# Two halves of 272 columns for the fourth query tile's selected and compressed keys

## The chip, the cores and the metric

The kernel runs on one core of one Trainium2 chip. The metric is the device time of one execution in microseconds (us); the time quoted for a kernel is the median of its runs. The profile comes from one further execution. Its engines are PE (matrix multiplication), PEld (loading of PE's stationary operand), DVE (vector engine), ACT (scalar engine), POOL (GpSimd) and SP (which issues most transfers).

## The reference

One decoder layer over 512 tokens of width 2048: a mixer with two head groups, cross attention over 256 memory tokens, and a SwiGLU. The change lies in the first head group, sparse attention with 8 query heads and 2 key/value heads. Each head attends to compressed blocks (31 of them), to selected blocks, and to a sliding window, with a distance penalty on each score. Cut to these three branches:

```python
s = jnp.einsum('bkgtd,bknd->bkgtn', qb, kc)                  # compressed
s = jnp.where(vis, s - sl5 * (t[:, None] - cmp_mid[None, :]), NEG)
p = jax.nn.softmax(s, axis=-1)
o_cmp = jnp.einsum('bkgtn,bknd->bkgtd', p, vc)
...
s = jnp.einsum('bkgtd,bktnsd->bkgtns', qb, ks_g)             # selected
s = jnp.where(ok, s - sl6 * (tt - pos), NEG)
o_slc = softmax over (n, s) of s, times vs_g
...
s = jnp.einsum('bkgtd,bksd->bkgts', qb, kw)                  # window
o_win = softmax of the masked s, times vw
return gb[..., 0:1] * o_cmp + gb[..., 1:2] * o_slc + gb[..., 2:3] * o_win
```

With 512 tokens, the 16 selected blocks of 64 are all 8 that exist and the window of 512 reaches every earlier token, so both branches are causal attention with different keys.

## The kernel before

**Number format.** Each fp32 operand is split into a high and a low part (`split`, line 158: ACT casts the high part, DVE subtracts it from the original to get the low one). A product is three matmuls: high x high, high x low, low x high (`mm3`).

**Query tiles.** The 512 tokens are four tiles of 128 (`i` from 0 to 3). Tile `i` sees `n = 128 * (i + 1)` keys of the selected branch (`b == 0`, in the tiles KS) and of the window branch (`b == 1`, in KV). The 32 columns ahead of the selected keys in KS hold the compressed keys. Tiles 0 to 2 get both from one product of 160, 288 and 416 columns. For tile 3 that would be 544 columns, and one PSUM bank holds 512; so its selected keys are one product of 512 columns, and its compressed keys a product of 32 that shares tile 0's bank.

**Behind each product.** ACT has written the scaled distances into the tile P beforehand (line 738). DVE adds them to the scores and takes the row minimum in one instruction (line 750, with a read of its accumulator), scales the minimum (751), and ACT takes the exponential with a row sum (752). For the compressed columns, DVE adds their distances and writes `pc` (`visible`, line 711). When all four tiles are through, `weigh_blocks` makes the compressed softmax (714 to 720), and `scale` multiplies P by the gate over the row sum (730). Later PE transposes P (775), ACT and DVE split it into PH and PL, and PE multiplies them with the values into the bank named o.

**Order.** PE runs what it is given in a fixed order, and two things make that order. In the program, work that has to wait runs as generators (`flows`): a generator says after how many ticks it goes on, and the projections of the dense stream tick, once per six matmuls of 512 columns. Head h is started by its projection (two projections of 8 ticks each pass per head: one of queries, one of gates), waits until head h - 1 is done scoring, and then yields two ticks per score tile (one in the last head), eight tiles in all. Its attention products wait for those of head h - 1. Behind the last two gate products (`w_r67`), `flows.drain()` lets what is still open run to its end; then comes the output projection, whose first two tiles (`begun`) are taken up to their fifteenth of sixteen products before the sixteenth, that of head 7. Then a scheduler places every instruction on its engine, by priority and by when it takes its inputs to be ready, so that the matmuls of the output projection stand between those of the drain.

**Banks.** PSUM's eight banks are three named mm, two s, two t and one o. Scores go to the two named s in turn.

**Transfers.** The sums of blocks of w_down are DMAs on POOL's queue (lines 143 and 145); each goes out at a fixed tick (`SUMS`). POOL also reloads head and gate tiles that were spilled (line 844, into KS buffers), and SP's queue loads the weights (188) and x (852).

Of the kernel before, what the change touches and what calls it, by code (L numbers as in the profile page):

```python
# [14 lines left out]
OP = mybir.AluOpType  # L15
AX = mybir.AxisListType

T = 512
# [41 lines left out]
def hybrid_block(ctx: ExitStack, tc: tile.TileContext, x_t, mem_t, sv, cmat, umask, w_a, w_r67, w_v, w_vg, w_v3,  # L60
                 w_vsw, w_gk2, w_c1, w_c2, w_out, w_cq, w_ck, w_cv, w_co, w_gu, w_down, y_t):
    nc = tc.nc
    V, S, G, PE = nc.vector, nc.scalar, nc.gpsimd, nc.tensor
# [11 lines left out]
    def sb(shape, tag, bufs, dt=F32):  # L75
        return (pool_b if tag in LATE else pool).tile(shape, dt, name=tag, tag=tag, bufs=bufs)

    def small(tag, bufs):
        return sb([128, 32], tag, bufs)

    def triple(tag):
        return small(tag, 2)[:, :3 * NT].rearrange("p (a i) -> p a i", i=NT)
# [4 lines left out]
    def bank(tag):  # L87
        return psp.tile([128, 512], F32, name=tag, tag=tag, bufs={"mm": 3, "s": 2, "t": 2, "o": 1}[tag])
# [3 lines left out]
    def row(tag, dt=F32):  # L92
        return sb([128, 512], tag, BUFS[tag], dt)
# [3 lines left out]
    def mm(*args, **kw):  # L97
        last_mm[0] = PE.matmul(*args, **kw)  # L98
# [56 lines left out]
    def split(hi, lo, src, gain=None):  # L155

        if gain is None:
            return S.copy(hi, src), V.tensor_sub(lo, src, hi)  # L158
        return (S.activation(hi, src, AF.Copy, scale=gain),
                V.scalar_tensor_tensor(lo, src, gain, hi, op0=OP.mult, op1=OP.subtract))  # L160
# [38 lines left out]
    def mm3(ps, lhs, rhs, start, stop, again=False):  # L199
        mm(ps, lhs[0], rhs[0], start=start, stop=False, skip_group_check=again)  # L200
        mm(ps, lhs[0], rhs[1], start=False, stop=False, skip_group_check=again)
        mm(ps, lhs[1], rhs[0], start=False, stop=stop, skip_group_check=again)

    def part(pair, a, n):
        return pair[0][:, a:a + n], pair[1][:, a:a + n]
# [25 lines left out]
    def inv_rms(dst, src, n, tmp):  # L231

        S.activation(dst, src, AF.Ln, bias=eps, scale=1.0 / n)
        S.activation(dst, dst, AF.Exp, scale=-0.5)
        S.activation(tmp, dst, AF.Square)
        V.scalar_tensor_tensor(tmp, src, n * EPS, tmp, op0=OP.add, op1=OP.mult)
        V.tensor_scalar(tmp, tmp, -0.5 / n, 1.5, op0=OP.mult, op1=OP.add)
        V.tensor_mul(dst, dst, tmp)
# [317 lines left out]
    for h in range(GH):  # L556
        qk = []
        flows.start(gla_head(h, qk))
        q, k = row("Q"), row("Q")
# [68 lines left out]
    keys = [[None, None], [None, None]]  # L628
# [49 lines left out]
    def nsa_head(h, ps):  # L678
        kv = h // 4
        slope = 2.0 ** -(h + 1)  # L680
        qn = row("Q", F32R), row("Q", F32R)
        split(*qn, ps, g_q)
        sq = row("n")
        S.activation(sq, ps, AF.Square)
        yield W_SUM
        pn = bank("s")
        for i in range(NT):
            mm(pn[:, i:i + 1], sq[:, 128 * i:128 * i + 128], one, start=True, stop=True)
        qs = triple("qs")
        sc, sl, neg = qs[:, 0], qs[:, 1], qs[:, 2]  # L690
        V.tensor_mul(neg, pn[:, :NT], rc2)
        inv_rms(sc, neg, 128, sl)
        V.tensor_mul(sc, sc, rc)
        V.reciprocal(sl, sc)
        V.tensor_scalar(sl, sl, slope, None, op0=OP.mult)
        V.tensor_scalar(neg, sc, -1.0, None, op0=OP.mult)
        yield W_NORM
        while not {"kc", ("k", 0, kv), ("k", 1, kv)} <= done or h and ("s", h - 1) not in done:
            yield 1
        sm = triple("sm")  # L700
        mn = triple("mn")
        cf = triple("cf")

        def coefficients(b):
            V.reciprocal(cf[:, b, :], sm[:, b, :])
            V.tensor_mul(cf[:, b, :], cf[:, b, :], gates[:, :, 3 * h + b])

        pc, pc3 = sb([128, NT, 32], "pc", 1), sb([128, NT, 3, 32], "pc3", 1)

        def visible(i, s):  # L710
            V.scalar_tensor_tensor(pc[:, i], cdist[:, 32 * i:32 * i + 32], sl[:, i:i + 1], s, op0=OP.mult, op1=OP.add)

        def weigh_blocks():
            V.tensor_reduce(mn[:, 0, :], pc, axis=AX.X, op=OP.min)
            V.tensor_sub(pc, mn[:, 0, :][:, :, None].to_broadcast([128, NT, 32]), pc)
            V.tensor_mul(pc, pc, sc[:, :, None].to_broadcast([128, NT, 32]))
            S.activation(pc, pc, AF.Exp)
            V.reduce_sum(sm[:, 0, :], pc, axis=AX.X)
            coefficients(0)
            V.tensor_mul(pc3, pc[:, :, None, :].to_broadcast([128, NT, 3, 32]),  # L720
                         cf[:, 0, :][:, :, None, None].to_broadcast([128, NT, 3, 32]))

        ps_ = []

        def scale(b):
            coefficients(1 + b)
            for i in range(NT):
                n = 128 * (i + 1)
                pi = ps_[b][:, POFF[i]:POFF[i] + n]
                V.tensor_scalar(pi, pi, cf[:, 1 + b, i:i + 1], None, op0=OP.mult)  # L730

        for b in range(2):
            p = sb([128, 1280], "P", 2)
            ps_.append(p)
            for i in range(NT):
                n = 128 * (i + 1)
                pi = p[:, POFF[i]:POFF[i] + n]
                S.activation(pi, dist[:, 512 - n:], AF.Copy, scale=sl[:, i:i + 1])
                s = bank("s")
                q = part(qn, 128 * i, 128)  # L740
                c = 32 if b == 0 and i < 3 else 0
                mm3(s[:, :c + n], q, part(keys[b][kv], 0 if b or c else 32, c + n), start=True, stop=True)
                if c and i == 0:
                    mm3(s[:, 160:192], part(qn, 384, 128), part(keys[0][kv], 0, 32), start=True, stop=True)
                    visible(3, s[:, 160:192])
                if c:
                    visible(i, s[:, :32])
                s = s[:, c:c + n]
                m = mn[:, 1 + b, i:i + 1]
                V.tensor_tensor_reduce(pi, s, pi, scale=1.0, scalar=3e38, op0=OP.add, op1=OP.min, accum_out=m)  # L750
                V.tensor_mul(m, m, sc[:, i:i + 1])
                S.activation(pi, pi, AF.Exp, bias=m, scale=neg[:, i:i + 1], accum_out=sm[:, 1 + b, i:i + 1])
                yield 2 if h < NH - 1 else 1
            if b == 0:
                weigh_blocks()
            scale(b)
        done.add(("s", h))

        while "vc" not in done or h and ("a", h - 1) not in done:
            yield 1  # L760
        pct = bank("t")
        for i in range(NT):
            PE.transpose(pct[:96, 128 * i:128 * i + 128], pc3[:, i].rearrange("p r n -> p (r n)"), ident)
        pcs = row("e", F32R)[:96]
        S.copy(pcs, pct[:96])
        V.tensor_sub(pcs[64:], pct[64:96], pcs[64:])
        o = None
        for b in range(2):
            pt = sb([128, 1280], "PH", PTB, F32R), sb([128, 1280], "PL", PTB, F32R)

            def turn(j):
                n = 128 * (NT - j)
                tp = bank("t")
                for i in range(j, NT):
                    PE.transpose(tp[:, 128 * (i - j):128 * (i - j) + 128],
                                 ps_[b][:, POFF[i] + 128 * j:POFF[i] + 128 * j + 128], ident)
                split(*part(pt, TOFF[j], n), tp[:, :n])

            def weigh(j):
                n = 128 * (NT - j)  # L780
                mm3(o[:, 128 * j:], part(vsw[j], 256 * b + 128 * kv, 128), part(pt, TOFF[j], n),
                    start=False, stop=b == 1 and j == NT - 1)

            turn(0)
            yield 2
            if b == 0:
                o = bank("o")
                mm(o, vc[:, 128 * kv:128 * kv + 128], pcs, start=True, stop=False)
            for j in range(1, NT):
                turn(j)  # L790
                weigh(j - 1)
                yield 2
            weigh(NT - 1)
        done.add(("a", h))
        t = row("st" if h < 4 else "M")
        S.copy(t, o)
        sq = row("on")
        S.activation(sq, t, AF.Square)
        pn = yield from column_sums(sq, T, "on", "t", W_SUM)
        r = row("on")  # L800
        inv_rms(r, pn, 128, row("on"))
        V.scalar_tensor_tensor(t, t, vec("g_nsa"), r, op0=OP.mult, op1=OP.mult)
        mix[h] = spill(t) if h < 4 else t
# [294 lines left out]
    for j in range(8):  # L1098
# [5 lines left out]
        for k, i in order if j < 7 else sorted(order, key=lambda o: o[1]):  # L1104
            kt = 2 * j + k
            mm3(acc_v[i], part(mem["v"][kt], 128 * i, 128), part(halves[j], 512 * k, 512),
                start=kt == 0, stop=kt == KT - 1)
# [568 lines left out]
```

## Time and profile before

| | |
|---|---|
| runs | 2321.61, 2326.07, 2322.61 us; median 2322.61 |
| profiled execution | 2317.59 us, its span 2315.8 |
| sparse-attention scores | 365.3 to 670.2 us of the span (line 750) |
| granted PE clock, mean | 0.999 |

A span is the time from the first to the last instruction. PE's matmuls overlap: an instruction's length holds its way through the array, so the distance from one start to the next is what a matmul costs. In the views below, L98 is the line at which every matmul is recorded; what it computes is told by the tile it writes (s: scores, o: attention output, t: transposes and sums, mm: projections).

### The profile page before, as it was taken

The page shows a single profiled execution, that of the slowest core. Times are in us where ns is not written, and L with a number is a line of the kernel's source. Part 1 is how long each engine was busy: PE and PEld are TensorE (multiplying, and loading weights), DVE is VectorE, ACT ScalarE, POOL GpSimd, SP SyncE. Part 2 cuts the span into 40 slices and gives each one's busy share as a digit, 9 for nine tenths or more (in the row PEclk, how much of TensorE's full clock was granted, in tenths as well). Part 3 has the DMA queues.
Part 4 walks back from the last instruction along what each step waited for, and adds up shares of the span by engine and source line. Part 5 has one row for each costly group of instructions (what it writes and reads, how often), then busy time and mean ns, then how long its engine had stood idle before and what let it go on. Part 6 is the DMA issues. An engine that isn't in the chain of part 4 may idle for free.

```text
span 2315.8 us, 29653 instructions
## 1 busy us (share of the span) xinstructions
PE 2291.5 (99%) x10868; PEld 1906.0 (82%) x10868; DVE 1676.3 (72%) x2556; ACT 1188.2 (51%) x1825; POOL 151.4 (7%) x224
## 2 busy tenths in 40 slices
PE   8999999999999999999999999999999999999999
PEld 7988888888888878778888888888888888888787
DVE  6477765677784436688888788878887876775685
ACT  6334444566673335575455445545554555444442
POOL 0011101011111100120000000000000000000000
PEclk9999999999999999999999999999999999999999
DMA  6576656466658754495455435544554497666674
GB/s 195 140 182 161 155 163 176 119 178 174 153 171 249 197 166 146 169 255 180 151 168 178 158 123 174 175 150 139 173 177 141 146 329 273 243 238 243 244 256 146
DMA packets 138018, 425.79 MB, mean 184 GB/s; under 512 B 14192, under 2 KB 34672, under 8 KB 134544
## 3 DMA queue, kind: packets, MB, share of 16 engines
q1 hardware_dynamic: 80752, 306.96, 39.1%
q0 software_dynamic: 31392, 88.36, 15.9%
q10 hardware_dynamic: 25728, 28.58, 3.5%
q8 instruction: 85, 1.39, 0.2%
q14 instruction: 61, 0.50, 0.1%
HBM read 382.42 MB, written 85.72 MB: 202 GB/s over the span
## 4 chain that ended last, share of the span: by engine, by line
PE 50%; DMA 2%; DVE 2%; issue 1%; ACT 0%; SPq 0%; DVEq 0%; POOLq 0%; ACTq 0%
PE mm L98 20%; PE t L98 13%; PE s L98 9%; PE o L98 7%; DMA raw<-w_down 1%; DVE ql L158 1%; PE s L1315 1%; DMA raw<-w_gu 1%; DMA raw<-td 0%; DMA PB<-h 0%; DVE raw L1453 0%; PE t L1484 0%; ACT qh L158 0%; DVE C L1494 0%; DVE C L1407 0%
## 5 line engine op out<-in xcount | busy, mean ns | idle before, releaser
L158 ACT CAST qh<-raw 128x1024 fp32r<-128x1024 f32 (+1 forms) x526 | 511.6, 981 | 542.5 <-PE o L98 165.1
L158 DVE TENSOR_TENSOR ql<-raw,qh 128x1024 fp32r<-128x1024 f32 (+1 forms) x526 | 591.7, 1133 | 142.4 <-PE mm L98 49.9
L98 PE MATMUL mm<-X,wh 128*128 128x512 f32 x1600 | 506.2, 396 | 0.0
L98 PEld LDWEIGHTS mm<-X,wh 128*128 128x128 f32 x1600 | 295.0, 189 | 56.7 <-issue 0.8
L98 PE MATMUL t<-qh,PB 128*128 128x512 f32 x968 | 335.8, 392 | 0.1
L98 PE MATMUL mm<-X,wl 128*128 128x512 f32 x800 | 314.4, 393 | 0.1
L98 PE MATMUL mm<-qh,PB 128*128 128x512 f32 x868 | 310.1, 390 | 0.2 <-DVE C L1494 0.2
L158 DVE TENSOR_TENSOR wl<-w,wh 128x1024 fp32r<-128x1024 f32 (+2 forms) x150 | 179.6, 1200 | 161.4 <-ACT wh L158 159.8
L158 ACT CAST wh<-w 128x1024 fp32r<-128x1024 f32 (+2 forms) x150 | 154.1, 1029 | 234.6 <-PE mm L98 168.3
L98 PE MATMUL s<-qh,PB 128*128 128x512 f32 x672 | 233.1, 391 | 1.0 <-DVE T L1494 0.9
L98 PE MATMUL mm<-qh,PA 128*128 128x512 f32 x640 | 221.8, 390 | 0.0
L98 PEld LDWEIGHTS t<-qh,PB 128*128 128x128 f32 x968 | 181.8, 188 | 37.7 <-DVE C L1409 0.8
L98 PEld LDWEIGHTS mm<-qh,PB 128*128 128x128 f32 x868 | 163.0, 188 | 34.4 <-DVE C L1494 0.6
L98 PE MATMUL t<-ql,PB 128*128 128x512 f32 x484 | 188.8, 390 | 1.1 <-DVE ql L158 1.1
L98 PE MATMUL o<-qh,PB 128*128 128x512 f32 x484 | 187.8, 390 | 0.0
L98 PEld LDWEIGHTS mm<-X,wl 128*128 128x128 f32 x800 | 150.8, 188 | 32.7 <-DVE wl L158 1.4
L98 PE MATMUL mm<-ql,PB 128*128 128x512 f32 x434 | 169.5, 391 | 3.7 <-DVE ql L158 3.7
L98 PEld LDWEIGHTS s<-qh,PB 128*128 128x128 f32 x672 | 126.1, 188 | 27.5 <-DVE T L1494 1.3
L98 PEld LDWEIGHTS mm<-qh,PA 128*128 128x128 f32 x640 | 120.2, 188 | 25.1
L98 PE MATMUL s<-ql,PB 128*128 128x512 f32 x336 | 131.4, 391 | 0.1
L98 PE MATMUL mm<-ql,PA 128*128 128x512 f32 x320 | 124.6, 389 | 0.0
L1230 DVE TENSOR_TENSOR raw<-raw 128x1024 f32<-128x1024 f32 x80 | 97.0, 1222 | 15.8 <-DMA raw<-w_gu 15.8
(488 smaller groups left out, 3462.0 us busy)
## 6 DMA issues: line engine op xcount, KB each, us to landing
raw<-w_gu SPq DMA_DIRECT2D x88, 768.0 KB, 4.2
raw<-w_gu SPq DMA_DIRECT2D x88, 512.0 KB, 3.4
raw<-w_down SPq DMA_DIRECT2D x88, 512.0 KB, 4.6
td<-w_down POOLq DMA_DIRECT2D x66, 512.0 KB, 6.6
w<-w_a SPq DMA_DIRECT2D x60, 512.0 KB, 4.2
raw<-td SPq DMA_DIRECT2D x22, 1024.0 KB, 4.8
PB<-h POOLq DMA_DIRECT2D x35, 512.0 KB, 4.6
h<-T ACTq DMA_DIRECT2D x66, 256.0 KB, 3.3
```

The source lines that it names most:

```text
L98: last_mm[0] = PE.matmul(*args, **kw)
L158: return S.copy(hi, src), V.tensor_sub(lo, src, hi)
L1230: V.tensor_sub(raw[:, 0:1024], raw[:, 0:1024], raw[:, 512:1536])
L1315: PE.transpose(ps[f][:, 128 * i:128 * i + 128], hs[i][:, c:c + 128], ident)
```

## The change

Tile 3 of the selected branch no longer has a product of its own for the compressed keys. Its 32 + 512 columns are cut into two products of 272 columns each, in two banks, with a yield of one tick between them. The first half holds the 32 compressed keys and the first 240 selected ones, the second half the other 272. DVE reduces each half by itself, the second into a new column `most`, and a minimum of the two follows. Tiles 0 to 2 and the window branch are computed as before.

```diff
@@ -700,6 +700,7 @@
         cf = triple("cf")
+        most = small("most", 1)
 
@@ -736,18 +737,25 @@
                 S.activation(pi, dist[:, 512 - n:], AF.Copy, scale=sl[:, i:i + 1])
-                s = bank("s")
                 q = part(qn, 128 * i, 128)
-                c = 32 if b == 0 and i < 3 else 0
-                mm3(s[:, :c + n], q, part(keys[b][kv], 0 if b or c else 32, c + n), start=True, stop=True)
-                if c and i == 0:
-                    mm3(s[:, 160:192], part(qn, 384, 128), part(keys[0][kv], 0, 32), start=True, stop=True)
-                    visible(3, s[:, 160:192])
-                if c:
-                    visible(i, s[:, :32])
-                s = s[:, c:c + n]
+                c = 0 if b else 32
                 m = mn[:, 1 + b, i:i + 1]
-                V.tensor_tensor_reduce(pi, s, pi, scale=1.0, scalar=3e38, op0=OP.add, op1=OP.min, accum_out=m)
+                cuts = (0, c + n) if c + n <= T else (0, 272, c + n)
+                for j, (x, y) in enumerate(zip(cuts, cuts[1:])):
+                    if j:
+                        yield 1
+                    s = bank("s")
+                    mm3(s[:, :y - x], q, part(keys[b][kv], x, y - x), start=True, stop=True)
+                    z = 0 if j else c
+                    if z:
+                        visible(i, s[:, :z])
+                    if j:
+                        least, m = m, most[:, :1]
+                    V.tensor_tensor_reduce(pi[:, x + z - c:y - c], s[:, z:y - x], pi[:, x + z - c:y - c],
+                                           scale=1.0, scalar=3e38, op0=OP.add, op1=OP.min, accum_out=m)
+                    if j:
+                        V.tensor_tensor(least, least, m, op=OP.min)
+                        m = least
                 V.tensor_mul(m, m, sc[:, i:i + 1])
                 S.activation(pi, pi, AF.Exp, bias=m, scale=neg[:, i:i + 1], accum_out=sm[:, 1 + b, i:i + 1])
                 yield 2 if h < NH - 1 else 1
```

The change adds 8 lines above what follows it, so line 750 of before is 754 after, 711 is 712, 751 is 759 and 818 is 826.

On PE, at the score tiles of head 0 (s: the score bank, KS: the keys, Q: the queries; rows with - stand in before only, with + in the changed kernel only), the first tile:

```order
 L98 MATMUL mm<-wh,X 128x512
 L98 MATMUL s<-KS,Q 128x160 x3
-L98 MATMUL s<-KS,Q 128x32 x3
 L98 MATMUL o<-wh,X 128x512
 L98 MATMUL o<-wl,X 128x512
```

The three small products of tile 3's compressed keys are gone from tile 0's bank. On PE, at the fourth tile of the same head:

```order
 L98 MATMUL mm<-wl,X 128x512
 L98 MATMUL mm<-wh,X 128x512
-L98 MATMUL s<-KS,Q 128x512 x3
+L98 MATMUL s<-KS,Q 128x272 x3
 L98 MATMUL o<-wh,X 128x512
 L98 MATMUL o<-wl,X 128x512
```

The first half stands where the product of 512 columns stood; the second half follows one tick later, behind six more matmuls of the dense stream, and everything behind it in the head moves by that tick.

On DVE, behind the last two gate products (q<-mm), in the drain, before the change (P: scores of the last head, mn: row minima, wl: low part of a weight tile, X: low part of a tile of the output projection's input):

```order
L818 TENSOR_TENSOR q_6276<-mm,rs 128x512
L818 TENSOR_TENSOR q_6286<-mm,rs 128x512
L158 TENSOR_TENSOR wl<-w,wh 128x1024
L750 ISA P,mn<-s,P 128x128
L750 ISA mn 128x1
L750 ISA P,mn<-s,P 128x256
L750 ISA mn 128x1
L751 TENSOR_TENSOR mn<-mn,qs 128x1
L158 TENSOR_TENSOR X<-KS,X 128x512
L751 TENSOR_TENSOR mn<-mn,qs 128x1
L750 ISA P,mn<-s,P 128x384
```

And at the same place in the changed kernel (pc: scores of the compressed keys):

```order
L826 TENSOR_TENSOR q_6250<-mm,rs 128x512
L158 TENSOR_TENSOR X<-M,X 128x512
L826 TENSOR_TENSOR q_6260<-mm,rs 128x512
L158 TENSOR_TENSOR wl<-w,wh 128x1024
L754 ISA P,mn<-s,P 128x128
L754 ISA mn 128x1
L754 ISA P,mn<-s,P 128x256
L754 ISA mn 128x1
L759 TENSOR_TENSOR mn<-mn,qs 128x1 x2
L712 SCALAR_TENSOR_TENSOR pc<-cm,qs,s 128x32
L754 ISA P,mn<-s,P 128x384
L754 ISA mn 128x1
```

The scores that stand behind the gate products were those of the last head's window branch; now they are those of its selected branch (the row that writes pc belongs to that one), and the window branch follows further down.

## The prediction

> **What bounds the kernel now.** I read the page first, for the busy shares and the chain of work that ended last.
>
> ```profile
> span 2315.8 us, 29653 instructions
> ...
> PE 2291.5 (99%) x10868; PEld 1906.0 (82%) x10868; DVE 1676.3 (72%) x2556; ACT 1188.2 (51%) x1825; POOL 151.4 (7%) x224
> ...
> PE 50%; DMA 2%; DVE 2%; issue 1%; ACT 0%; SPq 0%; DVEq 0%; POOLq 0%; ACTq 0%
> ```
>
> PE is the bound nearly everywhere, so an edit pays by the PE time that it takes out, and costs whatever PE then has to wait for. The average says nothing on the sparse-attention stage itself, so next I read the busy time of each engine in stretches of it.
>
> ```profile
> core 0: us, PE busy (x) PEld busy (x) DVE busy (x) ACT busy (x) POOL busy (x), PEclk, DMA share, GB/s
> 620.00:650.00 30.00, 30.00 (x162) 25.38 (x162) 22.91 (x72) 21.75 (x49) 3.94 (x6) 1.00 0.53 141
> 650.00:660.00 10.00, 9.90 (x53) 8.00 (x52) 8.38 (x29) 7.51 (x20) 1.07 (x2) 1.00 0.31 109
> 660.00:670.00 10.00, 10.00 (x50) 7.99 (x49) 9.69 (x25) 7.86 (x17) 2.68 (x5) 1.00 0.61 204
> 670.00:680.00 10.00, 10.00 (x53) 8.13 (x52) 9.45 (x23) 9.56 (x22) 1.08 (x2) 1.00 0.66 221
> 680.00:690.00 10.00, 10.00 (x57) 8.00 (x56) 7.71 (x16) 7.38 (x15) 0.00 (x0) 1.00 0.30 99
> ```
>
> PE has no gap (the columns are length, then busy time and count by engine), and its clock is granted in full. But while DVE has a quarter of its time free until 650, it is 94 to 97% busy from 660 to 680, and ACT nearly as much from 670. That is the drain: the projections that PE used as filler end at 665, and the last two heads finish beside the first output products. The stage has room for DVE work in its middle, and little at its end.
>
> **The change: PE.** Per head, three matmuls of 512 columns and three of 32 go; six of 272 come. PE's prices are distances between starts, since the matmuls overlap; so I read its timeline around two score blocks of one head (columns: start, length, engine, line, what, count).
>
> ```profile
> 640.93 0.60 PE L775 MATMUL t<-ident,P 128*128 128x128 f32 x4
> 641.29 0.82 PE L98 MATMUL s<-KS,Q 128*128 128x160 f32 x6
> 641.96 0.72 PE L98 MATMUL mm<-X,wh 128*128 128x512 f32 x2
> ...
> 642.75 0.62 PE L98 MATMUL mm<-X,wh 128*128 128x512 f32 x2
> 643.20 0.39 PE L98 MATMUL mm<-X,wl 128*128 128x512 f32 x1
> 643.42 0.56 PE L98 MATMUL s<-KS,Q 128*128 128x288 f32 x3
> 643.82 0.64 PE L98 MATMUL mm<-X,wh 128*128 128x512 f32 x2
> ...
> 656.20 0.45 PE L98 MATMUL s<-KV,Q 128*128 128x128 f32 x3
> 656.49 0.45 PE L98 MATMUL mm<-X,wl 128*128 128x512 f32 x1
> ```
>
> Three of 512 columns take 642.75 to 643.42, 0.225 us each; three of 288 take 0.40, 0.133 each; three of 128 take 0.29, 0.097 each. The row of six at 641.29 holds three of 160 columns and the three of 32, in 0.67. Between 128 and 288 columns 160 comes to 0.106, which leaves 0.117 for each of 32 columns: they cost as much as 128. 272 columns, by the slope between 288 and 512 (0.00041 a column), cost 0.126. A head so pays 3 x 0.225 + 3 x 0.117 = 1.03 us before and 6 x 0.126 = 0.76 after. The saving is 0.27 a head, **2.1 us** for eight; 1.7 if 32 columns cost only the 0.097 of 128.
>
> The Trainium skill, "TensorE: Matmul & The Clock Gate", section "Back-to-back issue gap", speaks against it: it gives columns / 2.4 GHz + 2.5 ns, with a floor of about 25 ns for small ones. By that rule the three small matmuls cost 0.075 us, a head saves under 0.03, and an estimate for the whole is 0.2 us. The six in 0.67 us disagree with it: by its own price of 69 ns for 160 columns, the three of 32 would still take 0.46.
>
> **The change: DVE.** One reduction of 512 columns becomes two, of 240 and 272, each with a read of its accumulator, and a minimum of two columns is added. The groups of DVE in the stage price it (count, then busy sum and mean ns).
>
> ```profile
> L750 DVE CUSTOM_DVE_ANT_0 P<-s,P 128x512 f32<-128x512 f32 x16 | 11.0, 686 | 0.8 <-ACT P L738 0.7
> L751 DVE TENSOR_TENSOR mn<-mn,qs 128x1 f32<-128x1 f32 x64 | 10.0, 157 | 1.3
> ...
> L750 DVE CUSTOM_DVE_ANT_0 P<-s,P 128x384 f32<-128x384 f32 x16 | 8.9, 554 | 2.2 <-PE s L98 2.1
> ...
> L711 DVE SCALAR_TENSOR_TENSOR pc<-cm,qs,s 128x32 f32<-128x32 f32 x32 | 7.4, 240 | 4.1 <-PE s L98 3.8
> ...
> L750 DVE CUSTOM_DVE_ANT_0 P<-s,P 128x256 f32<-128x256 f32 x16 | 6.7, 419 | 1.9 <-PE s L98 1.9
> ```
>
> From 256 to 512 columns a reduction grows by 267 ns, so it has 152 ns that don't depend on width. The split costs that once more, the minimum 157 and the read of the accumulator 84 (below): 0.39 us a head. For seven heads DVE's free quarter hides it; in the last it lies in the drain and is counted there. The four visibility rows (L711) stay four.
>
> The new wait: nine banks named s are taken where eight were, from two, and the second half's follows the first by one tick instead of two. PE's weight loads stand behind it. The view of line 750 says what that wait is worth.
>
> ```profile
> L750 DVE DVE_READ_ACCUMULATOR2_ANT mn<- x64: 76/84/91, 365.5 to 670.2; 128x1 f32 x64
> ...
>   PEld s L98: 2.9, 12
> ```
>
> 2.9 us in 12 waits over 64 banks. At the same 0.045 a bank eight more cost 0.4; nothing at best; at worst 0.24 a wait in each head, 1.9. I take **+0.4**, since the loads run ahead of PE.
>
> **The change: ticks.** The program counts filler in ticks, six matmuls of 512 columns each; a head yields two ticks per score tile. The added yield makes a head 17 ticks where two projections give 16, and head h+1 starts scoring when head h is done. Counting the yields, head 7 starts 6 ticks later (395, not 389), while the projections end at tick 400 either way; the drain has 30 ticks, not 24. So 36 matmuls, 8.1 us, no longer lie beside the last head. In the drain the order of DVE above shows it: behind the last gate product only head 7's window scores were left; now most of its selected scores stand there too. The trace of before prices the drain from that product (L818) to the last of head 7's transposed low parts (PL at 689.24).
>
> ```profile
> 665.00 1.29 DVE L818 TENSOR_TENSOR q<-mm,rs 128x512 f32<-128x512 f32 x2
> 666.19 1.22 DVE L158 TENSOR_TENSOR wl<-w,wh 128x1024 fp32r<-128x1024 f32 x1
> 667.33 0.29 DVE L750 CUSTOM_DVE_ANT_0 P<-s,P 128x128 f32<-128x128 f32 x1
> ...
> 672.61 1.27 DVE L730 TENSOR_SCALAR P<-P,cf 128x128 f32<-128x128 f32 x4
> 673.80 1.21 DVE L158 TENSOR_TENSOR wl<-w,wh 128x1024 fp32r<-128x1024 f32 x1
> ...
> 689.24 0.28 DVE L158 TENSOR_TENSOR PL<-t,PH 128x128 fp32r<-128x128 f32 x1
> ```
>
> ```profile
> 665.00:689.50 24.50, 24.50 (x130) 19.86 (x128) 21.35 (x50) 21.55 (x45) 2.59 (x5) 1.00 0.54 182
> ```
>
> The order of after has 38 DVE rows more between these two: five reductions with their reads and column products 2.3 us (starts lie 0.08 closer than lengths), four scalings 1.2 (672.61 to 673.80), four splits of 512 columns 2.4 (0.60 each, as at 665.00), one weight split 1.1, three low parts 1.3, and the compressed branch's softmax and coefficients about 2.0, an estimate from L711 and columns. That is 10.3 us. PE has 11 filler matmuls more (2.5), fifteen score matmuls (2.0), nine of attention (1.3, at the score prices) and eight transposes (0.7, at the 0.09 of 640.93): 6.5 us. So PE needs 24.5 + 6.5 = 31.0, and DVE 21.35 + 10.3 = 31.65. DVE becomes the bound of the drain. If none of its 3.15 idle us stay, PE waits 0.65; if all do, 3.8. I take **+3.0**: DVE and ACT hand each block back and forth, both are over 87% busy, so the idle time between hand-overs is more likely to stay.
>
> Behind the drain comes head 7's norm, which ends in the split that the sixteenth product of two output tiles reads.
>
> ```profile
> 691.98 1.23 DVE L158 TENSOR_TENSOR wl<-w,wh 128x1024 fp32r<-128x1024 f32 x1 [1.26 <-PE mm L98]
> 693.13 0.68 DVE L158 TENSOR_TENSOR on<-on 128x512 fp32r<-128x512 f32 x1
> ```
>
> PE has 38 matmuls of cover there, 8.6 us, where it had 43. The chain loses as much: the weight split that held DVE until 693.13 has moved ahead of it. Zero, up to 1.1 if the split is late again.
>
> **The change: transfers.** The sums of w_down on POOL's queue go out at fixed ticks, so behind the drain each goes out 6 ticks earlier against the work. One now stands ahead of the last two reloads of spilled tiles (KS). By the prices above, DVE uses these some 8 us after their buffers come free, and they land in 2.9.
>
> ```profile
> td<-w_down POOLq DMA_DIRECT2D x5, 512.0 KB, 5.6
> td<-td POOLq DMA_DIRECT2D x4, 512.0 KB, 8.2
> KS<-spill POOLq DMA_DIRECT2D x6, 256.0 KB, 2.9
> ```
>
> Even queued behind a whole copy of 5.6 they are just in time: zero, at most 0.5. On SP's queue a load of x moves ahead of two of w_out that aren't read before the drain's end: zero. The memory-key stage, where PE does wait, meets copies and sums in another phase.
>
> ```profile
> 800.00:820.00 20.00, 17.88 (x77) 14.20 (x76) 7.11 (x7) 6.29 (x6) 2.23 (x3) 1.00 0.76 211
> 820.00:840.00 20.00, 17.24 (x73) 13.71 (x72) 8.72 (x15) 9.20 (x26) 1.68 (x2) 0.91 0.60 178
> ```
>
> PE is idle 2.1 + 2.8 = 4.9 us there. As many transfers fall into it as before; I take zero, between -4.9 (it vanishes) and +2.6 (one sum of 8.2 in place of a copy of 5.6).
>
> **The sum.** -2.1 + 0.4 + 3.0 = **+1.3 us**. The profiled execution took 2317.59, so 2318.9 for its like; the median of the runs is 2322.61, so I predict **2323.9**. The measurement can tell 0.2%, 4.6 us, from no change: below 2318.0 is faster, above 2327.3 slower.
>
> **Rivals.**
> - The saving stands alone: DVE works without gaps in the drain and no bank is waited for: -2.1 + 0.65 = -1.5, 2321.2. For it: 75% load ahead of the drain, so DVE arrives with nothing owed. Against it: ACT's 21.55 of 24.50.
> - The cover that is lost is lost in full: the order on PE is fixed, and in it head 7's first transposes and products now follow each other with no filler between, so all 36 matmuls of cover come back as waits: -2.1 + 0.4 + 8.1 = +6.4, 2329.0, **slower**. It decides once the drain's wait passes 6.3 us. For it: DVE at 97% from 660; against it: DVE's own sum asks for 3.8 at most.
> - The change doesn't do what it says: 272 columns don't hide the weight load, and each matmul costs the 0.188 of a load's mean, which the page has.
>
> ```profile
> L98 PEld LDWEIGHTS s<-qh,PB 128*128 128x128 f32 x672 | 126.1, 188 | 27.5 <-DVE T L1494 1.3
> ```
>
>   Then a head pays 1.13, not 0.76: +0.8 in place of -2.1, +4.2 in all, 2326.8. Against it: 0.133 for 288 columns in the same place.
> - The shifted sums clear the memory-key stage and the drain holds: -1.5 - 4.9 = -6.4, 2316.2, faster. Against it: the transfers there are as many.
>
> **How the numbers follow.** The forecast has 0.47, the saving alone 0.22, the unhidden loads 0.06; all three lie within 0.2%: same 0.75. Lost cover 0.16 is slower, the cleared stage 0.09 faster. The range runs from 2319.5 (the saving alone, less 1.7, half of what the highest of the runs, 2326.07, lies above their median) to 2329.0, the price of lost cover; it leaves out the cleared stage and the part of lost cover beyond its price.
>
> **What would show it.** Score rows of 272 columns about 0.126 us apart, with none of 32. DVE over 95% busy in the 30 us behind the last gate product, and PE idle for 1 to 4 us there, before DVE's low parts or ACT's casts. If PE is idle for over 6, the lost cover is right; if for none, the saving alone. The memory-key stage should still be idle for about 5; if it isn't, the prediction falls by a cause beside the drain.

## The result, and the profile after

The changed kernel takes 2339.77 us (median of five runs, 2338.16 to 2344.15) against 2322.61: 1.008 times the time of the kernel before, interval 1.0068 to 1.0091. It is slower by some 17 us; 2323.9 was predicted, and 2329.0 was the end of the range. Its profiled execution has this page (span, then busy time by engine):

```profile
span 2337.5 us, 29690 instructions
...
PE 2306.4 (99%) x10868; PEld 1909.3 (82%) x10868; DVE 1675.8 (72%) x2580; ACT 1189.6 (51%) x1825; POOL 151.7 (6%) x224
```

The span is 21.7 us longer, and PE, with as many matmuls, is busy for 14.9 of them. So most of the loss is not idle time: the matmuls themselves are longer, or stand further apart. The steps that were predicted come first.

**The scores.** The timeline of PE at the two halves of head 0's fourth tile:

```profile
376.85 0.53 PE L98 MATMUL s<-KS,Q 128*128 128x272 f32 x3
377.22 0.40 PE L98 MATMUL o<-wh,X 128*128 128x512 f32 x1
...
378.61 0.54 PE L98 MATMUL s<-KS,Q 128*128 128x272 f32 x3
378.99 0.39 PE L98 MATMUL mm<-wh,X 128*128 128x512 f32 x1
```

Three matmuls of 272 columns take 0.37 and 0.38 us, that is about 0.125 each, where 0.126 was predicted. The 272-column step is right.

**The drain.** Busy time in its stretches (columns as before: length, then each engine, granted clock, transfers):

```profile
660.00:670.00 10.00, 10.00 (x53) 8.38 (x53) 8.02 (x15) 5.84 (x11) 0.00 (x0) 1.00 0.16 53
670.00:680.00 10.00, 8.79 (x45) 6.70 (x43) 8.97 (x37) 8.64 (x21) 1.91 (x4) 1.00 0.41 133
680.00:690.00 10.00, 7.85 (x43) 6.45 (x44) 8.47 (x27) 8.97 (x22) 1.84 (x4) 0.98 0.60 183
690.00:700.00 10.00, 10.00 (x44) 8.14 (x44) 6.98 (x12) 6.30 (x12) 1.08 (x2) 0.84 0.44 132
```

PE is idle for 1.21 + 2.15 = 3.36 us from 670 to 690, where it was busy throughout before. The waits of PE from 640 to 700 name them (total, times, longest); the same view of the kernel before has no row at all:

```profile
PE o L98 <- ACT X L158: 2.1, 1, 2.1
PE o L98 <- DVE PL L158: 1.4, 2, 1.2
```

The second row is a low part of P for which PE waits, as foreseen. The first row's releaser has to be checked, since a wait for several things is put down to the last. The timeline at its end (last column: idle time before the instruction, and who ended it):

```profile
687.04 1.27 DVE L731 TENSOR_SCALAR P<-P,cf 128x128 f32<-128x128 f32 x4
...
688.35 0.69 DVE L774 TENSOR_TENSOR e<-t,e 32x512 fp32r<-32x512 f32 x1
688.45 0.61 ACT L158 CAST X<-KS 128x512 fp32r<-128x512 f32 x1
...
689.18 0.47 PE L98 MATMUL o<-e,vc 96*128 96x512 f32 x1 [2.10 <-ACT X L158]
```

The matmul reads e. Its low part ends on DVE at 689.04, and ACT's cast of X happens to end at 689.06. So the wait is DVE's: the compressed branch's e stands in DVE's queue behind the four scalings of the window branch. And then something that no term of the sum had. The windows of 1 us around this wait (the clock granted to PE is the last number but two):

```profile
687.00:688.00 1.00, 0.08 (x1) 0.00 (x0) 0.96 (x5) 1.00 (x4) 0.29 (x1) 1.00 0.51 182
688.00:689.00 1.00, 0.00 (x0) 0.00 (x0) 0.97 (x2) 1.00 (x4) 0.00 (x0) 1.00 0.99 201
689.00:690.00 1.00, 0.82 (x5) 0.78 (x6) 0.97 (x3) 1.00 (x3) 0.00 (x0) 0.85 0.78 311
690.00:691.00 1.00, 1.00 (x4) 0.81 (x4) 1.00 (x3) 0.59 (x2) 0.35 (x1) 0.50 0.01 4
691.00:692.00 1.00, 1.00 (x3) 0.77 (x3) 1.00 (x2) 0.00 (x0) 0.19 (x1) 0.50 0.24 37
692.00:693.00 1.00, 1.00 (x4) 0.85 (x3) 0.02 (x1) 0.00 (x0) 0.45 (x1) 0.50 0.69 217
693.00:694.00 1.00, 1.00 (x8) 0.86 (x7) 0.00 (x0) 0.96 (x2) 0.08 (x1) 0.94 0.22 29
```

Behind 2.1 idle us the clock stands at 0.50 for 3.4 us, and PE does 3 or 4 matmuls per us in place of the 5 to 9 it did from 680 to 687. Added up, (1 - 0.85) + 3 x 0.50 + (1 - 0.94) = 1.7 us of clock are lost: the wait costs nearly twice its length.

**The memory-key stage.** Its windows, of the kernel before and then of the changed one:

```profile
800.00:960.00 160.00, 153.95 (x727) 127.23 (x726) 87.33 (x157) 78.46 (x151) 9.91 (x15) 0.99 0.47 148
```

```profile
800.00:960.00 160.00, 154.34 (x711) 126.67 (x710) 81.58 (x141) 72.53 (x137) 9.68 (x14) 0.99 0.49 150
```

PE is idle for 6.05 us before and 5.66 after. It is not the place.

**Where the time goes.** The start of the n-th matmul record can be compared between the profiles, since both have 10868 of them. How far the changed kernel lies behind, in us:

```
matmul        400   1600   3200   3600   4800   last
lag           1.7    3.3    8.3   13.8   17.6   21.7
before, at   79.6  291.6  606.5  683.9  950.2  2311.2
```

(The profiled execution of before lies 5.0 us under its median, so the last number is larger than the 17 of the medians. Behind matmul 4800, 3.1 of the 4.1 us come near 1045 us, where the clock of the changed kernel falls to one half for 3.41 us once more; the profile of before has no such spell there, but three kernels below that are as fast as before have one (256 idle bytes, both idle tiles, ticks shared out), so the change need not be its cause.) Three things are in this row. From 3200 to 3600, the drain, the lag grows by 5.5. But it has grown to 3.3 before the first score is multiplied (365 us), where the order of the instructions is the same, and it goes on growing behind the drain. So I looked at the distance of matmuls where both kernels do the same, near 20 us. Of the kernel before, the start of a product o<-wh,X and that of the one 12 matmuls later:

```profile
20.20 0.39 PE L98 MATMUL o<-wh,X 128*128 128x512 f32 x1
...
22.92 0.39 PE L98 MATMUL o<-wh,X 128*128 128x512 f32 x1
```

And of the changed kernel:

```profile
20.77 0.40 PE L98 MATMUL o<-wh,X 128*128 128x512 f32 x1
...
23.55 0.40 PE L98 MATMUL o<-wh,X 128*128 128x512 f32 x1
```

12 matmuls take 2.72 us before and 2.78 after, 0.227 and 0.232 each, at a clock of 1.00 in both. That holds for the matmuls of 512 columns that read X and the weight tiles wh and wl, the last of which starts at 904 us before and at 922 after; those behind, which read other tiles, are 227 ns apart in both kernels. The trace has 2784 of them. What can touch them all is where the tiles lie. The added tile `most` takes 128 bytes per partition in the pool that wh and wl come from; it moved wh from address 134016 to 133888, that is from 128 bytes past a multiple of 256 to a multiple of 256, and wl likewise. X, in another pool, stayed at 128 bytes past one.

### The profile page after: what moved, and what is told of

The parts are those of the page before. It is cut to its first block, busy times and chain, and to the rows that moved or that the text cites. A ratio compares the mean times of both kernels' runs of the same rounds, so it can differ in the third digit from the quotient of the medians.

```text
span 2337.5 us, 29690 instructions
## 1 busy us (share of the span) xinstructions
PE 2306.4 (99%) x10868; PEld 1909.3 (82%) x10868; DVE 1675.8 (72%) x2580; ACT 1189.6 (51%) x1825; POOL 151.7 (6%) x224
## 4 chain that ended last, share of the span: by engine, by line
PE 91%; DVE 3%; DMA 2%; ACT 2%; issue 2%; ACTq 0%; SPq 0%; POOL 0%; DVEq 0%; POOLq 0%
PE mm L98 50%; PE t L98 15%; PE s L98 14%; PE o L98 9%; PE s L1323 1%; DMA w<-w_out 1%; PE t L783 1%; DVE ql L158 1%; ACT wh L158 1%; DVE wl L158 1%; DMA w<-w_ck 0%; DMA raw<-w_gu 0%; DMA w<-w_c 0%; ACT P L760 0%; DMA PB<-h 0%
## 5 line engine op out<-in xcount | busy, mean ns | idle before, releaser
L98 PE MATMUL mm<-X,wh 128*128 128x512 f32 x1600 | 511.8, 400 | 0.0
```

## The experiments

Two theories were to be told apart, and what each is worth: **the address** (the tile `most`, through the place of wh and wl) and **the order** (the split, and the tick between its halves). Ratios are to the kernel before, run on the same chip; its medians there were 2320.7 to 2321.6.

**Order without address.** The changed kernel, with `most` taken from an unused column of mn, so that no tile moves:

```diff
-        mn = triple("mn")
+        mn = small("mn", 2)
+        most = mn[:, 12:13]
+        mn = mn[:, :12].rearrange("p (a i) -> p a i", i=NT)
         cf = triple("cf")
-        most = small("most", 1)
...
-                        least, m = m, most[:, :1]
+                        least, m = m, most
```

> The changed kernel with its column for the second minimum taken from the unused end of the tile mn, so that no tile is added and every other tile stands at the address it had before the change; the order on each engine is that of the changed kernel. Address theory (the added tile moves one pool by 128 bytes, and matmuls that read it step at 232 ns instead of 227): about 14 us come back, 2324 to 2327 us, matmuls of 512 columns 227 ns apart in the first 950 us, and what is left, 1 to 5 us over before, is the drain. Order theory (all of the loss is the new order: drain, banks, transfers): 2338 to 2341 us, 232 ns apart as in the changed kernel.

Measured: 2330.32 us, ratio 1.0039 (1.0025 to 1.0053); 512-column matmuls 227 ns apart again. About half of the loss is gone with the address, and the order costs about 9 us; the time lies between the two theories, so both things cost.

**Address without order.** The kernel before with the idle tile, and then with one of twice its size:

```diff
+        small("most", 1)
```

> The kernel before with a tile of 128 bytes per partition added in the same pool and read by nothing; no instruction differs. Address theory: 2335 to 2338 us (2,600 matmuls of 512 columns that read the weight tiles wh and wl, 5 ns each, is 13 to 14 us), 232 ns apart. Order theory: 2322 to 2323 us, 227 ns.

```diff
+        sb([128, 64], "most", 1)
```

> As the run before, but the idle tile has 256 bytes. If the place within 256 bytes is what counts, wh and wl are back at 128 beyond a multiple of 256, and the time is that of before, 2321 to 2325 us, at 227 ns. If a longer stretch counts (512 bytes or more), or any shift at all, it is slow: 2334 us or more, at 230 ns or more.

Measured: 2329.01, ratio 1.0033 (1.0021 to 1.0046), for 128 bytes; 2322.59, 1.0007 (0.9996 to 1.0019), for 256. A tile that nobody reads costs 7.4 us, if it moves the others by 128 bytes, and nothing if by 256. That is half of the 13 to 14 us that were expected. In the profiles the distances behind the 2784 matmuls that read X against wh or wl come to 661.4 us, against 654.6 with 256 bytes: 6.8 us more, near the 7.4. Their median grows by 5 ns, but their mean only by 2.5: with 256 bytes a third of them stood 228 ns apart or more already. The two ratios, 1.0039 and 1.0033, come to 1.0072, at the lower end of the interval of the whole change.

**Whose address.** The kernel before with an idle tile ahead of X in its pool; then with both idle tiles:

```diff
+    pool_b.tile([128, 32], F32, name="lead")
```

> The kernel before with an idle tile of 128 bytes at the head of the other pool, so that X (the other operand of most of these matmuls) moves to a multiple of 256 and wh and wl stay 128 beyond one. Theory 'the weights' own place counts': 2321 to 2325 us, 227 ns. Theory 'the two operands must lie alike within 256 bytes': slow, 2334 to 2338 us, 232 ns. Theory 'no operand may start at a multiple of 256': slow as well.

```diff
+    pool_b.tile([128, 32], F32, name="lead")
...
+        small("most", 1)
```

> The kernel before with both idle tiles, one of 128 bytes at the head of X's pool and one of 128 bytes in the pool of wh and wl; no instruction differs. X, wh and wl then all stand at multiples of 256 bytes (in the kernel before, X and the weight tiles alternate: X 128 beyond, wh at 128, wl at 128). Theory A, that the operands of a matmul must stand alike within 256 bytes: the 512-column matmuls step at 227 ns as in the kernel before, time 2321 to 2325. Theory B, that no operand may stand at a multiple of 256 bytes: they step at 232 or more, time 2329 to 2337. If each operand costs by itself, the pitch is above 232, about 237, and the time 2335 to 2340.

Measured: 2330.11, 1.0038 (1.0024 to 1.0052), with X moved alone (the 2334 and more that were expected rest on the same 13 to 14 us); 2320.93, 1.0001 (0.9991 to 1.0011), with X and the weights moved. The median distances, worked out from the traces, with the tiles' places within 256 bytes:

```
                         X    wh,wl  qh,ql   mm<-X,wh   mm<-X,qh
before                 128      128    128     227 ns     227 ns
changed                128        0    128     232        227
before + 128           128        0    128     232        227
before + 256           128      128    128     227        227
before, X moved          0      128    128     232        231
before, both moved       0        0    128     227        231
```

The last row settles it within one kernel: X at 0 is fast with weights at 0, and slow with qh at 128. Neither place is bad by itself; the two operands have to lie alike. The kernel before has a few that bear it out: M stands at 0, and the 24 matmuls of 512 columns that read it against wh or wl, at 128, have medians of 232.5 and 230.5 ns. For matmuls that read KV or KS no such difference stands out of their scatter, and shifts other than 128 were not tried.

**The tick, and the halves.** What the order costs can come from the tick, which makes a head 17 ticks long, or from the halves. The tick alone in the kernel before; the changed kernel (without the tile) with no tick between its halves; and with tile 3's two ticks shared out, so that a head has 16 again:

```diff
+                if b == 0 and i == 3:
+                    yield 1
                 s = bank("s")
```

> The kernel before with one yield of one tick ahead of tile 3's scores in the first branch, and nothing else: 512 and 32 columns as before, no added tile. Theory A (the tick): 2330 to 2334, that is the +8.7 of the run without the tile, and 1.6 us more because the saving on the columns isn't there. Theory B (the halves): 2321 to 2325, as the kernel before.

```diff
-                    if j:
-                        yield 1
```

> The changed kernel without the added tile (most lies in an unused column of mn) and without the added yield between the halves: tile 3's second half stands directly behind its first, and the flows get as many ticks as in the kernel before. Theory A, that the +8.7 us left over in the run without the tile come from the added tick (work of the last head pushed behind the last gate product): 2319 to 2323, the PE saving of 1.6 us remains, less a wait for the second bank. Theory B, that they come from the halves themselves (more DVE and PE rows per head, more rounds of the score banks): still 2328 to 2332.

```diff
-                yield 2 if h < NH - 1 else 1
+                yield 2 if h < NH - 1 and len(cuts) == 2 else 1
```

> The changed kernel without the added tile and with tile 3's two ticks shared out, one between the halves and one behind them, so that a head takes as many ticks as before, but for the last one, which takes one more. Theory A (the ticks of all heads together push work behind the last gate product): most of the 8.7 us go, about 2321 to 2325; what the last head's one further tick costs remains, at most 2 us. Theory B (the halves themselves): still 2328 to 2332.

> The same kernel as the run with tile 3's ticks shared out (no added tile, one tick between the halves and one behind), in more rounds: it should lie at 2319 to 2322, and the interval tells whether the 1.6 us of PE's saving are there (ratio 0.9993) or not (1.000 or more).

Measured: the tick alone 2329.82, 1.0046 (1.0031 to 1.0061); no tick 2325.57, 1.0020 (1.0009 to 1.0031); ticks shared out 2319.05, 1.0003 (0.9992 to 1.0013), and in the second measurement 2320.40, 0.9998 (0.9989 to 1.0006). The tick alone costs what the whole order costs; the halves with 16 ticks cost nothing that can be told from noise. The kernel with no tick lies between its two theories. The waits of PE with the tick alone, from 640 to 700, and two windows:

```profile
PE o L98 <- DVE PL L158: 2.0, 2, 1.8
PE mm L98 <- ACT X L158: 0.7, 1, 0.7
PE s L98 <- DVE mn L752: 0.2, 1, 0.2
```

```profile
670.00:675.00 5.00, 2.58 (x15) 1.69 (x13) 5.00 (x14) 2.97 (x7) 1.07 (x2) 1.00 0.18 52
675.00:680.00 5.00, 5.00 (x19) 3.99 (x18) 3.45 (x6) 2.34 (x5) 2.15 (x4) 0.66 0.74 234
```

The drain of the changed kernel again, without its halves: PE waits while DVE is busy for 5.00 of 5.00, and then has 0.66 of its clock for 5 us (1.7 us lost). With the ticks shared out the same stretch has no gap:

```profile
670.00:675.00 5.00, 5.00 (x24) 4.04 (x23) 4.36 (x13) 5.00 (x12) 0.54 (x1) 1.00 0.68 231
675.00:680.00 5.00, 5.00 (x31) 4.07 (x31) 4.86 (x10) 4.62 (x10) 0.54 (x1) 1.00 0.65 217
```

The last head has one tick more than before in that kernel too, and it costs nothing; so it is the ticks that add up over the heads. Halves directly behind each other cost 4.9 us by the medians: there PE waits for a score bank that DVE hasn't read yet, five times between 370 and 700, and once for a weight tile, 2.8 us together:

```profile
PE s L98 <- DVE mn L753: 1.5, 5, 0.3
PE mm L98 <- ACT wh L158: 1.3, 1, 1.3
...
```

The other 2 us were not located.

**A tick less.** If a tick costs time, one less might bring some. The kernel before with one tick fewer per head, and the changed kernel (without the tile) with the tick between the halves and none behind:

```diff
-                yield 2 if h < NH - 1 else 1
+                yield 2 if h < NH - 1 and (b or i < 3) else 1
```

> The kernel before with one tick after tile 3's scores in the first branch where it has two: 15 ticks per head, nothing else. Theory A (a tick per head more costs because the last head's work then ends behind the last gate product, where nothing covers it): a tick less can give back only what the kernel before itself loses there, 0 to 1 us by its profile (PE busy 419.44 of 420 us from 300 to 720), and takes cover from each head's own norms: 2320 to 2324. Theory B (each tick costs by itself, about 9 us a tick per head): 2312 to 2316.

```diff
-                yield 2 if h < NH - 1 else 1
+                if len(cuts) == 2:
+                    yield 2 if h < NH - 1 else 1
```

> The changed kernel without the added tile, with one tick between tile 3's halves and none behind them: 15 ticks per head. Theory A: as the run with the ticks shared out, 2319 to 2323, or some us more if tile 3's reductions then lie too near the block weights that wait for them. Theory B (each tick costs by itself): 2310 to 2314.

Measured: 2329.05, 1.0036 (1.0022 to 1.0050), and 2332.89, 1.0053 (1.0039 to 1.0067). Both theories fall here: with 15 ticks the kernel is 8.1 and 11.9 us slower; with 17 it was 9.1 and 8.7. The waits of the first, from 370 to 700, lie elsewhere, before score banks and weight parts:

```profile
PE s L98 <- DVE mn L750: 1.1, 3, 0.6
PE mm L98 <- DVE wl L158: 1.1, 2, 0.8
PE o L98 <- DVE PL L158: 0.5, 2, 0.2
PE o L98 <- DVE e L766: 0.2, 1, 0.2
```

So it isn't that later is worse. Two projections give a head 16 ticks; a head of 15 or 17 moves by one tick against the projections with each head, and each would come to its own collisions. That 16 is the good count was measured; that the step of the projections is why, is argued. The waits listed add up to some 3 us of 8; the rest is spread over distances that the view of waits doesn't count, and was not located.

## Why the prediction was wrong

**The step that failed** is "The change: DVE": it priced "a minimum of two columns is added" as 157 ns, and the column `most` that it needs at nothing; that it moves wh and wl by 128 bytes, and that this lengthens matmuls far from the change (2784 of 512 columns read X against them), was not weighed. Missing term: +7.4 us by the medians. It is not the whole of the miss: without it the changed kernel took 2330.3, still past the 2329.0 at the range's end. The rest is a second step, the +3.0 of "The change: ticks", for which the runs have some 9.

**The second step: the drain.** DVE's work there was added up rightly; that its total sets the time was wrong, and the term was too small. From the first of the last two gate products, at 667.6, to the last of head 7's low parts, at 705.3, DVE is busy for 31.85 us, where 31.65 stood. But the stretch is 37.7 us long, and DVE is idle for 5.85 of it, longest for a cast of ACT (2.25 us, up to 694.27). In the 30 us from 668.8 it is busy for 24.4, or 81%, where over 95% was to be the sign; so its total is not the bound. What PE waits for, 3.36 us in all, are low parts at two places where DVE has no gap (4.97 of 5.00 us from 675, 1.93 of 2 from 687) and takes other rows first. That size is within the 0.65 to 3.8 of the prediction, though it was reached from the total.

What the prediction left out is that a wait of 2 us halves PE's clock for 3.4 more: 1.7 us. From matmul 3200 to 3600 the changed kernel without the tile falls behind by 5.3 us (from 3.4 to 8.7 on the scale of the lag above), the tick alone by 4.9, where +3.0 stood. The "lost cover in full", priced at +8.1, comes near what the tick costs by the medians (+9.1), but not by its mechanism: PE is idle there for 3.4 us (2.9 with the tick alone), not 8.1. Up to the drain the tick costs another 1.6 us (its lag grows from 0.4 to 2.0), for which the sum has no term. That leaves some 2.6 of the 9.1 with no place shown for them. A part may lie in the memory-key stage: in the profiles of both kernels with 17 ticks and without the tile, the clock stands at one half for 6.83 us near 840, where it does for 3.41 before; that is 1.7 us more, but each is one execution.

**The rivals.** The unhidden weight load falls with the 0.125 us of the 272-column rows. The saving alone needed a drain without waits, which only the kernels with 16 ticks have.

**PE's saving** was put at 2.1. All distances behind such rows together are 7.88 us before (24 of 512 columns 5.56, 24 of 32 columns 2.32) and 6.32 after: 1.56. (Three of 512 columns in 0.67 us are 0.223 each, not 0.225; the forecast of 2.1 stays.) The 32 columns were priced at 0.117 each and take 0.097, the price of 128 columns that the prediction gave as the other bound. The rule of the Trainium skill, "TensorE: Matmul & The Clock Gate", section "Back-to-back issue gap", would have them at 0.025. But the section gives it for a single matmul by itself, and says that it under-counts small ones in a stream of weight loads and matmuls; the prediction took it for more than it states, and the trace has 0.097. In the kernel with shared ticks the 1.56 can't be told from nothing (0.9989 to 1.0006).

**The score banks**, +0.4: with a tick between the halves no wait of PE for a bank is listed; with none, 1.5. The term was small enough not to matter, and the yield is what keeps it so.

**The memory-key stage and the transfers**, zero: right, 5.66 idle us against 6.05.

## What to carry to other kernels

A new tile is part of a change's cost: compare the addresses of all tiles that PE reads before and after, and where two operands of one matmul no longer lie alike within 256 bytes, pad the tile (256 bytes cost nothing here) or take the space from an unused column. When every matmul of a kind is slower from the first microseconds on, at a full clock, look there and not at the edit. And where generators share a stream by ticks, keep the number of ticks per head when a step is split: split its ticks too.

## What the runs showed of the hardware

- Matmuls of 512 columns that read X against a weight tile are 227 ns apart in the median when both lie at the same place within 256 bytes, and 231 to 232 when they lie 128 bytes apart; 7.4 us of this kernel.
- The granted clock falls to one half when PE was idle for about half of a fixed stretch of 3.41 us. In the 13 profiles, leaving out the first 30 us and the last spell at the end, there are 27 such spells, 25 of 3.41 us and two of 6.83, and within a profile their starts lie a whole multiple of 3.413 us apart. In the stretch of that grid ahead of each spell, PE was idle for 1.75 us or more (by the modelled ends of its matmuls); in no other stretch for more than 1.85. So one wait of 1.76 us was enough (with the tick alone, ahead of 675.7) and the 2.10 above, and the 1.23 before PL, ahead of 680, was not; where a wait falls on the grid counts too. The Trainium skill, "TensorE: Matmul & The Clock Gate", section "Part 1: The HAM clock gate", has one half after an idle window of about 3.4 us, and the window free-running and 3413 ns long; the value of one half, the length of the spells and the grid agree, but half a window of idle time was enough here.
